# The experts of a gated trunk chosen one token tile after the other, and expert 0 gathered by itself

## The chip, the core and the metric

The kernel runs as one program on one core of a Trainium2 chip. The metric is the device time of an execution in microseconds. Five engines work from instruction queues of their own: TensorE (PE in the profile, with its weight loads shown as PEld), VectorE (DVE), ScalarE (ACT), GpSimd (POOL) and SyncE (SP), which issues nearly all of the transfers here. The DMA engines move the data.

## The reference

A decoder trunk of two layers on 256 tokens of width 1024. Layer 0 mixes tokens by forgetting attention, layer 1 by retention; after each mixer stands a mixture of experts, which is what the change is about. Its core:

```
def hier_moe(h, wr_g, br_g, wr_e, br_e, w_gu, w_down):
    p_group = softmax(xf @ wr_g + br_g)              # 4 groups
    pg, gi = top_k(p_group, 1)
    e_logits = (xf @ wr_e + br_e).reshape(T, 4, 8)   # 8 experts in each
    e_in = e_logits of the group gi
    pv, pi = top_k(softmax(e_in), 2)
    gates = pg * pv / sum(pv)
    expert_id = gi * 8 + pi
    return grouped_experts(...)   # (silu(x @ gate_e) * (x @ up_e)) @ w_down[e], times the gate, summed

for i in range(2):
    h = h + (forgetting_attention, retention)[i](rms_norm(h, norm_mix[i]), ...)
    hn = rms_norm(h, norm_ffn[i])
    h = h + hier_moe(hn, ...)
return rms_norm(h, norm_final)
```

All 32 experts of a layer have weights of their own, 6 MB each in float32 (4 MB for gate and up, 2 MB down), so that the expert weights of both layers are most of the 460 MB that the kernel reads.

## The kernel before

The 256 tokens are two tiles of 128 rows, t = 0 and 1. The residual stream `h` stays in SBUF as two tiles of 128 x 1024. The program is written in the order in which each engine runs it; nothing is scheduled afterwards.

Weights come through `Stream`: 26 slots of 1 MB, filled in a fixed order by SyncE (line 166). A load can be issued when a slot is free and the loads ahead of it have been issued; a slot is given back by the last instruction that reads it. The experts' loads stand in that list in the order of use, so that by the time a layer's gate is reached the slots hold the weights of experts 0 to 3 and a part of 4, and the next load needs a slot that expert 0 gives back. The first experts are cut into pieces of 1 MB: four for gate and up, two for down.

A layer's gate goes as follows. The last projection adds its halves to `h` (`add_h`, line 522). `Gate.transposes(n)` takes the squares of the rows on ScalarE (line 382), transposes `h` on TensorE (line 399) and copies it to `xg` (VectorE for tile 0, ScalarE for tile 1); for the second half it calls `row_rstd`, which forms 1/rms of both tiles: a sum (line 387) and a scaling (line 390) on VectorE and a power on GpSimd (line 391). `Gate.products(n)` multiplies by the router's weights (line 565) into one PSUM bank for both tiles. Then `phase_moe` starts. Nine matmuls of ones by ones (`keep_warm`, line 528) keep TensorE running. VectorE chooses the group and the two experts of each token (lines 927 to 944): logits, the largest eight, `match_replace` to mark the largest, equality, a mask over the experts of the other groups, the largest eight again, and `mkf`, the choice as zeros and ones. Each of these is written for tile 0 and tile 1 next to each other, and some are one operation for both. Three small matmuls (lines 946 to 948) count the tokens of each expert, `rk` (line 950) is the place of a token in its expert's list, and `one_hots(0)` (lines 954 and 956) makes matrices that pick up to 32 tokens for each of the four experts of a group, already scaled by rstd.

`gather` collects these rows: per half of the width two matmuls with a one-hot as the stationary operand and 512 columns of `h` (line 967), a copy on ScalarE (line 968), four transposes (line 974) and a multiplication by the norm's gain on VectorE (line 975). The result `xg` holds the inputs of the four experts side by side, 32 columns each.

Then the experts run one by one (`expert`): the gate and up product in four parts (line 1044, 16 matmuls a part), the activation on ScalarE (line 1053), its product on VectorE (line 1054), a transpose, and the down product (line 1072). Behind part 0 of expert 0 the gate values are computed (`gates`, lines 991 to 1008). The gather for the next group of four stands behind the third expert of a group.

Of the kernel before, what the change touches and what calls it, by code (L numbers as in the profile page):

```python
# [14 lines left out]
BF16 = mybir.dt.bfloat16  # L15
I32 = mybir.dt.int32
AF = mybir.ActivationFunctionType
ALU = mybir.AluOpType
# [209 lines left out]
def trunk(ctx, tc, x, fox_w_in, fox_b_f, fox_w_out, ret_w_in, ret_gn_gain, ret_w_out,  # L228
# [301 lines left out]
    class Gate:  # L530
# [3 lines left out]
        def __init__(self, l):  # L534
# [7 lines left out]
            self.top = r.new(2, 16)  # L542
            self.bank = None
            V.memset(self.L, BIG)

        def transposes(self, n):
# [10 lines left out]
            if n == 1:  # L557
                row_rstd()

        def products(self, n):  # L560
            if n == 0:
                self.bank = bank("pt")
            for t in range(2):
                for c in range(4):
                    mm(self.bank[:, 64 * t:64 * t + 36], self.xg[:, 4 * t + c, :],
                       wr[:, 4 * n + c, :], start=n == 0 and t == 0 and c == 0, stop=n == 1 and c == 3,
                       skip_group_check=True)


    def phase_a():  # L570
# [340 lines left out]
        g.products(1)  # L911
# [5 lines left out]
    def phase_moe(l, g, reserve_after, ahead, before_last, between):  # L917
# [3 lines left out]
        el, ng, rk, ex, den = r.new(2, 32), r.new(2, 4), r.new(2, NE), r.new(2, 37), r.new(2)  # L921
        gatef, gdiv, mc, gr, nrf, gs = r.new(2, NE), r.new(2, NE), r.new(1), r.new(7), r.new(1), r.new(4)
        mkf = cp.tile([P, 2, NE], BF16, name="mkf")
        keep_warm(9)
        for t in range(2):
            b = g.bank[:, 64 * t:64 * t + 36]
            V.scalar_tensor_tensor(L[:, t, 38:42], b[:, 0:4], rstd[:, t:t + 1], rb[:, 0:4], ALU.mult, ALU.add)
        for t in range(2):
            V.max(top[:, t, 8:16], L[:, t, 38:49])
        for t in range(2):  # L930
            b = g.bank[:, 64 * t:64 * t + 36]
            V.scalar_tensor_tensor(el[:, t, :], b[:, 4:36], rstd[:, t:t + 1], rb[:, 4:36], ALU.mult, ALU.add)
        for t in range(2):
            V.match_replace(Lr[:, t, 38:49], top[:, t, 8:16], L[:, t, 38:49], -BIG)
        V.tensor_tensor(ng, Lr[:, :, 38:42], L[:, :, 38:42], ALU.is_equal)
        for t in range(2):
            V.scalar_tensor_tensor(L[:, t, 0:32].rearrange("p (g e) -> p g e", g=4),
                                   ng[:, t, :, None].to_broadcast([P, 4, 8]), NEG,
                                   el[:, t, :].rearrange("p (g e) -> p g e", g=4), ALU.mult, ALU.add)
        for t in range(2):  # L940
            V.max(top[:, t, 0:8], L[:, t, 0:38])
        for t in range(2):
            V.match_replace(Lr[:, t, 0:38], top[:, t, 0:8], L[:, t, 0:38], -BIG)
        V.tensor_tensor(mkf, Lr[:, :, 0:32], L[:, :, 0:32], ALU.not_equal)
# [7 lines left out]
        def one_hots(g4):  # L952

            V.tensor_tensor(oh, rk[:, :, 4 * g4:4 * g4 + 4, None].to_broadcast([P, 2, 4, CAP]),
                            iota[:, None, None, :].to_broadcast([P, 2, 4, CAP]), ALU.is_equal)
            V.tensor_tensor(oh, oh, rstd[:, :, None, None].to_broadcast([P, 2, 4, CAP]), ALU.mult)  # L956
# [26 lines left out]
        one_hots(0)  # L983
        gather(g.xg, "acc", "acc")
# [280 lines left out]
    def phase_c():  # L1265
# [233 lines left out]
        g.products(1)  # L1499
# [78 lines left out]
```

## Time and profile before

| | us |
|---|---|
| median of three runs | 1248.16 |
| the three runs | 1246.19, 1248.60, 1248.16 |
| the profiled execution's own time | 1251.0 |
| its span in the profile | 1248.9 |
| TensorE busy in the span | 982.5 (79%) |
| VectorE busy | 414.3 (33%) |
| ScalarE busy | 317.6 (25%) |
| mean rate of the DMA over the span | 370 GB/s |

A profile is one execution. A busy share is an average over stages that have different limits: attention (0 to about 160 us), the first layer's experts (to about 590), retention (to about 806), the second layer's experts. So a change has to be read in its own stage. The releaser that stands behind an idle time is inferred: it is the event that came last.

### The profile page before, as it was taken

The numbers are of one execution on the slowest core, as the hardware profiler recorded it, in microseconds if no ns is written. First come the engines' busy times: TensorE is split into PE (matmuls) and PEld (weight loads), VectorE is DVE, ScalarE is ACT, GpSimd is POOL, SyncE is SP. The second block draws the span as 40 slices with busy tenths as digits, with TensorE's granted clock in tenths as the row PEclk, the third lists the DMA queues.
The fourth block names the chain that finished last, engine by engine and source line by source line (L and its number), as shares of the span: only waits on it lengthen the run. The fifth ranks groups of instructions, "written<-read, shape, count | busy, mean of one in ns | idle before, by whom it ended". The sixth has DMA issues, their size and how long they took to land.

```text
span 1248.9 us, 21544 instructions
## 1 busy us (share of the span) xinstructions
PE 982.5 (79%) x9223; PEld 634.3 (51%) x9223; DVE 414.3 (33%) x927; ACT 317.6 (25%) x672; POOL 42.8 (3%) x49
## 2 busy tenths in 40 slices
PE   8999986777575756678999999977776767677777
PEld 8888863343232323334889888744332323233333
DVE  5676832121111111111677676422121111111112
ACT  5665621111010100100554575321110111010112
POOL 2000000000000000000133100000000000000000
PEclk9999999899887879898999999989999888888979
DMA  9975879999999999999992768889999999999995
GB/s 339 321 264 192 321 279 421 419 427 426 427 426 427 428 428 426 427 426 394 378 335 69 268 237 308 332 357 419 423 427 428 427 427 427 427 427 427 428 424 192
DMA packets 74406, 462.20 MB, mean 370 GB/s; under 512 B 8881, under 2 KB 13761, under 8 KB 42050
## 3 DMA queue, kind: packets, MB, share of 16 engines
q1 hardware_dynamic: 73600, 460.17, 90.8%
q8 instruction: 74, 1.21, 0.4%
q10 hardware_dynamic: 706, 0.60, 0.2%
q14 instruction: 26, 0.21, 0.0%
HBM read 459.70 MB, written 1.05 MB: 369 GB/s over the span
## 4 chain that ended last, share of the span: by engine, by line
DMA 49%; PE 29%; DVE 2%; issue 1%; ACT 1%; POOLq 0%; ACTq 0%; SPq 0%; DVEq 0%
DMA slot<-in_expert_w_gu_dram 29%; DMA slot<-in_expert_w_down_dram 19%; PE sc L1044 5%; PE acc L495 4%; PE acc L509 3%; PE acc L507 3%; PE acc L508 3%; PE o L1072 3%; PE sc L967 1%; PE acc L1098 1%; DMA slot<-in_ret_w_in_dram 1%; DVE slot L1087 1%; PE pt L528 0%; PE acc L1138 0%; ACT slot L1085 0%
## 5 line engine op out<-in xcount | busy, mean ns | idle before, releaser
L1044 PE MATMUL sc<-slot,slot 128*32 128x256 f32 x4096 | 277.4, 422 | 54.9 <-DMA slot<-in_expert_w_gu_dram 51.8
L1044 PEld LDWEIGHTS sc<-slot,slot 128*32 128x32 f32 x4096 | 138.5, 119 | 181.4 <-issue 69.6
L1072 PE MATMUL o<-slot,slot 128*32 128x256 f32 x1984 | 137.8, 422 | 101.4 <-DMA slot<-in_expert_w_down_dram 58.7
L1072 PEld LDWEIGHTS o<-slot,slot 128*32 128x32 f32 x1984 | 70.8, 119 | 164.8 <-issue 80.2
L1054 DVE TENSOR_TENSOR slot<-slot,sc 128x128 f32<-128x128 f32 x64 | 23.7, 371 | 388.2 <-ACT slot L1053 388.2
L462 DVE SCALAR_TENSOR_TENSOR slot<-slot,gT,slot 128x512 fp32r<-128x512 f32 x160 | 123.9, 794 | 52.3 <-ACT slot L451 50.9
L495 PE MATMUL acc<-slot,slot 128*128 128x256 f32 x960 | 125.8, 288 | 1.6 <-ACT slot L451 1.1
L451 ACT ACTIVATE slot<-slot,gT 128x512 fp32r<-128x512 f32 x160 | 111.4, 718 | 38.6 <-PE acc L495 15.4
L495 PEld LDWEIGHTS acc<-slot,slot 128*128 128x128 f32 x960 | 118.9, 193 | 4.2 <-ACT slot L451 1.7
L1087 DVE COPY slot<-o 32x256 f32<-32x256 f32 x124 | 51.8, 418 | 204.3 <-PE o L1072 177.1
L1085 ACT ACTIVATE slot<-o 32x256 f32<-32x256 f32 x124 | 46.5, 375 | 281.5 <-DVE slot L1087 281.5
L1053 ACT ACTIVATE slot<-sc 128x128 f32<-128x128 f32 x64 | 17.7, 277 | 374.4 <-PE sc L1044 374.4
L507 PE MATMUL acc<-slot,slot 128*128 128x512 f32 x256 | 102.5, 400 | 0.0
L508 PE MATMUL acc<-slot,slot 128*128 128x512 f32 x256 | 100.0, 391 | 2.1 <-DVE slot L462 2.1
L509 PE MATMUL acc<-slot,slot 128*128 128x512 f32 x256 | 100.1, 391 | 0.0
L967 PE MATMUL sc<-h,slot 128*128 128x512 f32 x112 | 72.8, 811 | 33.5 <-DVE slot L956 33.5
L1098 PE MATMUL acc<-slot,slot 128*128 128x512 f32 (+1 forms) x128 | 60.9, 611 | 13.4 <-ACT slot L1085 13.2
L967 PEld LDWEIGHTS sc<-h,slot 128*128 128x128 f32 x112 | 27.7, 258 | 74.6 <-issue 74.6
L508 PEld LDWEIGHTS acc<-slot,slot 128*128 128x128 f32 x256 | 48.2, 188 | 11.8 <-DVE slot L462 2.8
L509 PEld LDWEIGHTS acc<-slot,slot 128*128 128x128 f32 x256 | 48.0, 188 | 10.2
L507 PEld LDWEIGHTS acc<-slot,slot 128*128 128x128 f32 x256 | 48.2, 188 | 9.3 <-issue 0.3
L975 DVE TENSOR_TENSOR slot<-pt,gT 128x512 f32<-128x512 f32 x28 | 19.4, 691 | 96.5 <-PE pt L974 96.5
(237 smaller groups left out, 750.6 us busy)
## 6 DMA issues: line engine op xcount, KB each, us to landing
slot<-in_expert_w_gu_dram SPq DMA_DIRECT2D x84, 2048.0 KB, 39.1
slot<-in_expert_w_gu_dram SPq DMA_DIRECT2D x86, 1024.0 KB, 13.4
slot<-in_expert_w_down_dram SPq DMA_DIRECT2D x42, 2048.0 KB, 39.1
slot<-in_expert_w_down_dram SPq DMA_DIRECT2D x40, 1024.0 KB, 13.3
slot<-in_ret_w_in_dram SPq DMA_DIRECT2D x24, 1024.0 KB, 14.1
slot<-in_fox_w_in_dram SPq DMA_DIRECT2D x15, 1024.0 KB, 11.8
slot<-in_ret_w_out_dram SPq DMA_DIRECT2D x8, 1024.0 KB, 7.3
slot<-in_fox_w_out_dram SPq DMA_DIRECT2D x4, 1024.0 KB, 14.6
```

What stands on the lines that cost most here:

```text
L451: A.activation(wh, w, AF.Copy, scale=1.0 if g is None else g)
L462: V.scalar_tensor_tensor(wl, w, g, wh, ALU.mult, ALU.subtract)
L495: mm(o, w[:, P * j:P * j + P], x[:, k, :], start=first and k == 0 and j % 2 == 0, stop=last and k == 7, skip_group_check=True)
L507: mm(banks[t], xh[:, q], wh, start=first and k == ks[0], stop=False)
L508: mm(banks[t], xh[:, q], wl, start=False, stop=False)
L509: mm(banks[t], xl[:, q], wh, start=False, stop=last and k == ks[-1])
L967: mm(b, o[:, t, :], h[:, t, 512 * n:512 * n + 512], start=t == 0, stop=t == 1)
L1044: mm(bgu[32 * j:32 * j + 32, 0:256].rearrange("p (two f) -> p two f", two=2), xg[:, kk, 32 * e4:32 * e4 + 32], wv[:, :, P * j:P * j + P], ...
L1072: mm(by[32 * nb:32 * nb + 32, 0:256], gTt[:, 32 * j:32 * j + 32], w[:, j % n, 256 * nb:256 * nb + 256], start=j == 0, stop=j == 3, skip_gr ...
L1085: A.activation(o, i, AF.Copy)
L1087: V.tensor_copy(o, i)
L1098: mm(sums[t, n], w2["scm"][0:rows, P * t:P * t + P], y4[0:rows, 512 * n:512 * n + 512], start=start, stop=False, skip_group_check=True)
```

## The change

There are three parts, the same in both layers.

The choice of experts moves from `phase_moe` into the gate and goes tile by tile. The router's products of the two tiles go to two PSUM banks. Where the last half of `h` is multiplied, the order is now: products of tile 0, rstd of tile 0 (`tile_rstd`, operations on one column), the group of tile 0, rstd of tile 1, the experts of tile 0, products of tile 1, the group and the experts of tile 1. Of the nine `keep_warm` matmuls ahead of the count six are left, in another bank.

Expert 0 gets an input of its own, `x0`: two one-hots of 32 columns, and sixteen matmuls that take a strided block of `h` as the stationary operand and give the transposed rows at once; VectorE multiplies them by the gain, one half of the width after the other. The one-hots of experts 1 to 3 follow.

The gather of the whole group is moved behind expert 0's gate and up product, ahead of its down product.

```diff
+    def tile_rstd(t):
+        V.tensor_tensor(st_[:, t:t + 1], ss[:, 0, t:t + 1], ss[:, 1, t:t + 1], ALU.add)
+        V.tensor_scalar(st_[:, t:t + 1], st_[:, t:t + 1], 1.0 / D, EPS, ALU.mult, ALU.add)
+        G.tensor_tensor(rstd[:, t:t + 1], st_[:, t:t + 1], mhalf[:, 0:1], ALU.pow)
...
-        g.products(1)
+        g.products(1, (0,))
+        tile_rstd(0)
+        g.groups(0)
+        tile_rstd(1)
+        g.experts(0)
+        g.products(1, (1,))
+        g.groups(1)
+        g.experts(1)
...
-        keep_warm(9)
...
+        keep_warm(6, "acc")
         b = bank("sc")
         mm(b[:, 0:32], trb, mkf[:, 0, :], start=True, stop=True, skip_group_check=True)
         mm(b[:, 32:64], onb, mkf[:, 0, :], start=False, stop=False, skip_group_check=True)
         mm(b[:, 32:64], trb, mkf[:, 1, :], start=False, stop=True, skip_group_check=True)
-        keep_warm(3)
+        keep_warm(3, "acc")
...
-        one_hots(0)
-        gather(g.xg, "acc", "acc")
+        x0 = g.xg[:, 0:2, :].rearrange("p a (k s) -> p (a k) s", s=CAP)
+        for t in range(2):
+            V.tensor_scalar(oh[:, t, 0, :], iota, rk[:, t, 0:1], rstd[:, t:t + 1], ALU.is_equal, ALU.mult)
+        bx = bank("acc")[:, 0:8 * CAP].rearrange("p (k s) -> p k s", k=8)
+        for n in range(2):
+            for c in range(4):
+                for t in range(2):
+                    hv = h[:, t, 512 * n:512 * n + 512].rearrange("p (q c) -> p c q", c=4)
+                    mm(bx[:, 4 * n + c, :], hv[:, c, :], oh[:, t, 0, :], start=n == 0 and c == 0 and t == 0,
+                       stop=t == 1, skip_group_check=True)
+            V.tensor_tensor(x0[:, 4 * n:4 * n + 4, :], bx[:, 4 * n:4 * n + 4, :],
+                            gT[:, gi, 4 * n:4 * n + 4, None].to_broadcast([P, 4, CAP]), ALU.mult)
+        one_hots(0, 1)
...
-            gg, gTt = first_product(e, e4, xg, after_part)
+            gg, gTt = first_product(e, e4, xg if e else x0, after_part)
             turned(gg, gTt)
+            if e == 0:
+                gather(xg, "acc", "acc")
             by = bank("o")
```

VectorE's row at the end of attention, from rstd to the choice of experts, before (`st_` is the mean square, `top`, the logits and the marks are parts of one slot):

```order
L387 TENSOR_TENSOR st__85<-ss 128x2
L390 TENSOR_SCALAR st__85<-st__85 128x2
L927 SCALAR_TENSOR_TENSOR slot_124<-pt,rstd,rb 128x4 x2
L929 MAX slot_124<-slot_124 128x8 x2
L932 SCALAR_TENSOR_TENSOR slot_124<-pt,rstd,rb 128x32 x2
L934 MATCH_REPLACE slot_124<-slot_124 128x11 x2
L935 TENSOR_TENSOR slot_124<-slot_124 128x8
L937 SCALAR_TENSOR_TENSOR slot_124<-slot_124 128x32 x2
L941 MAX slot_124<-slot_124 128x8 x2
L943 MATCH_REPLACE slot_124<-slot_124 128x38 x2
L944 TENSOR_TENSOR mkf<-slot_124 128x64
```

The same engine and place, now:

```order
L395 TENSOR_TENSOR st__85<-ss 128x1
L396 TENSOR_SCALAR st__85<-st__85 128x1
L577 SCALAR_TENSOR_TENSOR slot_124<-pt,rstd,rb 128x4
L578 MAX slot_124<-slot_124 128x8
L579 SCALAR_TENSOR_TENSOR slot_124<-pt,rstd,rb 128x32
L580 MATCH_REPLACE slot_124<-slot_124 128x11
L581 TENSOR_TENSOR slot_124<-slot_124 128x4
L395 TENSOR_TENSOR st__85<-ss 128x1
L396 TENSOR_SCALAR st__85<-st__85 128x1
L586 SCALAR_TENSOR_TENSOR slot_124<-slot_124 128x32
L589 MAX slot_124<-slot_124 128x8
L590 MATCH_REPLACE slot_124<-slot_124 128x38
```

Tile 0's choice (line 591) follows, and then the nine operations of tile 1, from line 577 to line 591 again; what stood in pairs stands in two rows one after the other.

TensorE's row from the count of tokens to expert 0's down product, before:

```order
L948 MATMUL sc<-mkf,trb 128x32
L528 MATMUL o<-ones 128x128 x3
L967 MATMUL acc<-h,slot_124 128x512 x4
L974 MATMUL acc<-ident,slot_124 128x128 x8
L987 LDWEIGHTS onb
L987 MATMUL sc<-mkf,onb 128x32
L988 LDWEIGHTS onb
L988 MATMUL sc<-mkf,onb 128x32
L1044 MATMUL sc<-slot_135,slot_124 32x256 x8
L1044 MATMUL sc<-slot_137,slot_124 32x256 x8
L1044 MATMUL sc<-slot_139,slot_124 32x256 x8
```

And now, with what each waits for, expert 0's narrow gather being line 1005 and its gate and up product line 1069:

```order
L959 MATMUL sc<-mkf,trb 128x32 [waits DVE_49]
L534 MATMUL acc<-ones 128x128 x3
L1005 MATMUL acc<-slot_124,h 128x32 [waits DVE_49] x2
L1005 MATMUL acc<-slot_124,h 128x32 x6
L1005 MATMUL acc<-slot_124,h 128x32 [waits DVE_49]
L1005 MATMUL acc<-slot_124,h 128x32 x7
L1012 LDWEIGHTS onb
L1012 MATMUL sc<-mkf,onb 128x32
L1013 LDWEIGHTS onb
L1013 MATMUL sc<-mkf,onb 128x32
L1069 MATMUL sc<-slot_135,slot_124 32x256 [waits DMAHW5_49,DMAHW1_49,PE_49]
L1069 MATMUL sc<-slot_135,slot_124 32x256 x7
```

The wide gather has left the row ahead of the first product, and the narrow one has a wait for VectorE at its ninth matmul, where its second half begins. Further on in the same row, behind the last part of expert 0's first product:

```order
L1069 MATMUL sc<-slot_989,slot_124 32x256 x7
L980 MATMUL acc<-h,slot_124 128x512 [waits DVE_49]
L980 MATMUL acc<-h,slot_124 128x512
L980 MATMUL acc<-h,slot_124 128x512 [waits PE_49]
L980 MATMUL acc<-h,slot_124 128x512
L987 MATMUL acc<-ident,slot_124 128x128 [waits Activation_49]
L987 MATMUL acc<-ident,slot_124 128x128 x3
L987 MATMUL acc<-ident,slot_124 128x128 [waits Activation_49]
L987 MATMUL acc<-ident,slot_124 128x128 x3
L1099 MATMUL o<-slot_991,slot_989 32x256 [waits DMAHW5_49,DVE_49]
L1099 MATMUL o<-slot_991,slot_989 32x256 x7
```

Here the wide gather (lines 980 and 987) stands now between expert 0's first product and its down product (line 1099).

## Rows read from the trace of the kernel before

**Rows 1.** Stages: length; busy PE, PEld, DVE, ACT, POOL; PEclk; DMA share; GB/s.
```profile
168.50:175.00 6.50, 6.22 (x46) 3.57 (x50) 1.66 (x5) 2.72 (x4) 0.00 (x0) 1.00 0.01 4
175.00:181.00 6.00, 4.80 (x92) 3.02 (x88) 2.92 (x14) 1.67 (x4) 0.00 (x0) 1.00 0.89 321
181.00:590.00 409.00, 282.95 (x3160) 142.18 (x3152) 66.01 (x160) 42.90 (x114) 0.00 (x0) 0.89 1.01 424
...
808.50:815.00 6.50, 6.22 (x54) 3.63 (x56) 2.03 (x8) 3.19 (x5) 0.00 (x0) 1.00 0.01 3
```

**Rows 2.** The chain that ended last, shares of the span by line.
```profile
DMA slot<-in_expert_w_gu_dram 29%; DMA slot<-in_expert_w_down_dram 19%; PE sc L1044 5%; PE acc L495 4%; PE acc L509 3%; PE acc L507 3%; PE acc L508 3%; PE o L1072 3%; PE sc L967 1%; PE acc L1098 1%; DMA slot<-in_ret_w_in_dram 1%; DVE slot L1087 1%; PE pt L528 0%; PE acc L1138 0%; ACT slot L1085 0%
```

**Rows 3.** Order of time, layer 0's gate: start us, us, instruction, [idle before <-releaser].
```profile
160.16 1.38 DVE L522 TENSOR_TENSOR h<-h,acc 128x512 f32<-128x512 f32 x2 [4.98 <-PE acc L509]
...
162.99 0.69 POOL L391 TENSOR_TENSOR rstd<-st__85,mhalf 128x2 f32<-128x2 f32 x1 [116.43 <-DVE st__85 L390]
...
164.25 0.35 DVE L927 SCALAR_TENSOR_TENSOR slot<-pt,rstd,rb 128x4 f32<-128x4 f32 x2 [1.44 <-PE pt L565]
...
165.04 0.08 DVE L934 MATCH_VALUE_LOAD slot<-slot 128x8 f32 x1
...
166.56 0.22 DVE L944 TENSOR_TENSOR mkf<-slot 128x64 bf16<-128x64 f32 x1
```

**Rows 4.** Order of time, from the rank to expert 0's first product.
```profile
167.24 0.23 DVE L950 SCALAR_TENSOR_TENSOR slot<-sc,mkf 128x64 f32<-128x64 f32 x1 [0.46 <-PE sc L948]
...
167.96 0.42 DVE L956 TENSOR_TENSOR slot<-slot,rstd 128x256 f32<-128x256 f32 x1
...
168.44 3.70 PE L967 MATMUL acc<-h,slot 128*128 128x512 f32 x8 [0.60 <-DVE slot L956]
...
173.36 0.11 PEld L987 LDWEIGHTS <-onb 128*128 128x128 bf16 x1
...
173.61 3.66 PE L1044 MATMUL sc<-slot,slot 128*32 128x256 f32 x64
```

**Rows 5.** SyncE's loads around expert 0, and one kind's size and count.
```profile
161.22 15.94 SPq L166 DMA_DIRECT2D slot<-in_expert_w_gu_dram  x4
179.59 2.05 SPq L166 DMA_DIRECT2D slot<-in_expert_w_down_dram  x2
...
slot<-in_expert_w_gu_dram SPq DMA_DIRECT2D x86, 1024.0 KB, 13.4
```

**Rows 6.** Order of time: the router's products, and the product behind the activation.
```profile
162.18 1.96 PE L565 MATMUL pt<-wr,slot 128*128 128x36 f32 x16
...
177.65 0.37 DVE L1054 TENSOR_TENSOR slot<-slot,sc 128x128 f32<-128x128 f32 x1 [0.50 <-ACT slot L1053]
```

**Rows 7.** GpSimd's power by line: count, ns min/median/max, first and last start, form.
```profile
L391 POOL TENSOR_TENSOR rstd<-st__85,mhalf x5: 693/699/1137, 19.6 to 1242.3; 128x2 f32<-128x2 f32 x5
...
L1363 POOL TENSOR_TENSOR rs<-rs,mhalf x8: 921/922/1066, 646.0 to 713.3; 128x1 f32<-128x1 f32 x8
```

**Rows 8.** Order of time: two operations of the gate values, each needing the last.
```profile
175.05 0.16 DVE L996 TENSOR_REDUCE slot<-slot 128x2 f32<-128x8 f32 x1 [0.33 <-ACT slot L995]
175.25 0.16 DVE L997 SCALAR_TENSOR_TENSOR slot<-slot 128x2 f32<-128x2 f32 x1
```

**Rows 9.** Order of time, layer 1: the choice, and expert 0's first product.
```profile
806.20 0.23 DVE L944 TENSOR_TENSOR mkf<-slot 128x64 bf16<-128x64 f32 x1
...
813.12 3.66 PE L1044 MATMUL sc<-slot,slot 128*32 128x256 f32 x64
```

**Rows 10.** Order of time: three of the fourteen gathers of later groups.
```profile
198.49 3.67 PE L967 MATMUL sc<-h,slot 128*128 128x512 f32 x8 [2.40 <-DVE slot L956]
...
245.74 5.37 PE L967 MATMUL sc<-h,slot 128*128 128x512 f32 x8 [2.40 <-DVE slot L956]
...
1163.30 5.37 PE L967 MATMUL sc<-h,slot 128*128 128x512 f32 x8 [2.40 <-DVE slot L956]
```

**Rows 11.** Stages, TensorE alone: length; PE busy; PEclk; DMA share; GB/s.
```profile
245.80:249.10 3.30, 3.30 (x4) 0.50 1.02 425
```

More of the change, by code (lines that the diff above doesn't have):

```diff
@@ L542, in __init__ @@
             self.top = r.new(2, 16)
+            self.el, self.ng = r.new(2, 32), r.new(2, 4)
+            self.mkf = cp.tile([P, 2, NE], BF16, name="mkf")
             self.bank = None
@@ L556, in transposes, with products, groups, experts @@
             h_transposed(n, "sc", evict)
-            if n == 1:
-                row_rstd()
-        def products(self, n):
+        def products(self, n, ts=(0, 1)):
             if n == 0:
-                self.bank = bank("pt")
-            for t in range(2):
+                self.bank = [bank("pt"), bank("o")]
+            for t in ts:
                 for c in range(4):
-                    mm(self.bank[:, 64 * t:64 * t + 36], self.xg[:, 4 * t + c, :],
-                       wr[:, 4 * n + c, :], start=n == 0 and t == 0 and c == 0, stop=n == 1 and c == 3,
-                       skip_group_check=True)
+                    mm(self.bank[t][:, 0:36], self.xg[:, 4 * t + c, :], wr[:, 4 * n + c, :],
+                       start=n == 0 and c == 0, stop=n == 1 and c == 3)
+        def groups(self, t):
+            L, Lr, top, b = self.L, self.Lr, self.top, self.bank[t]
+            V.scalar_tensor_tensor(L[:, t, 38:42], b[:, 0:4], rstd[:, t:t + 1], rb[:, 0:4], ALU.mult, ALU.add)
+            V.max(top[:, t, 8:16], L[:, t, 38:49])
+            V.scalar_tensor_tensor(self.el[:, t, :], b[:, 4:36], rstd[:, t:t + 1], rb[:, 4:36], ALU.mult, ALU.add)
+            V.match_replace(Lr[:, t, 38:49], top[:, t, 8:16], L[:, t, 38:49], -BIG)
+            V.tensor_tensor(self.ng[:, t, :], Lr[:, t, 38:42], L[:, t, 38:42], ALU.is_equal)
+        def experts(self, t):
+            L, Lr, top = self.L, self.Lr, self.top
+            V.scalar_tensor_tensor(L[:, t, 0:32].rearrange("p (g e) -> p g e", g=4),
+                                   self.ng[:, t, :, None].to_broadcast([P, 4, 8]), NEG,
+                                   self.el[:, t, :].rearrange("p (g e) -> p g e", g=4), ALU.mult, ALU.add)
+            V.max(top[:, t, 0:8], L[:, t, 0:38])
+            V.match_replace(Lr[:, t, 0:38], top[:, t, 0:8], L[:, t, 0:38], -BIG)
+            V.tensor_tensor(self.mkf[:, t, :], Lr[:, t, 0:32], L[:, t, 0:32], ALU.not_equal)
     def phase_a():
@@ L920, in phase_moe @@
         L, Lr, top, oh = g.L, g.Lr, g.top, g.oh
-        el, ng, rk, ex, den = r.new(2, 32), r.new(2, 4), r.new(2, NE), r.new(2, 37), r.new(2)
+        rk, ex, den = r.new(2, NE), r.new(2, 37), r.new(2)
         gatef, gdiv, mc, gr, nrf, gs = r.new(2, NE), r.new(2, NE), r.new(1), r.new(7), r.new(1), r.new(4)
-        mkf = cp.tile([P, 2, NE], BF16, name="mkf")
-        keep_warm(9)
[L925 to L944, printed above, removed]
+        mkf = g.mkf
+        keep_warm(6, "acc")
         b = bank("sc")
@@ L1498, in phase_c @@
         g.transposes(1)
-        g.products(1)
+        g.products(1, (0,))
+        tile_rstd(0)
+        g.groups(0)
+        tile_rstd(1)
+        g.experts(0)
+        g.products(1, (1,))
+        g.groups(1)
+        g.experts(1)
         yield g
```

10 lines of the change are left out of this document (6 added, 4 removed).

## The prediction

> **What bounds the kernel now.** I read the stages first [rows 1]. In the first expert phase (181 to 590 us; the second looks the same) the DMA share is 1.01 at 424 GB/s: expert weights arrive as fast as they can, TensorE is busy 283 of 409 us, and nothing that an engine does there moves the end. The projections ahead of each expert phase are not touched by the change. What remains are two short holes, one at the start of each expert phase: from 168.5 to 175 us and from 808.5 to 815 us the DMA moves 3 to 4 GB/s. There all slots are full, and the next load waits until expert 0's first product has used up a slot. The chain of waits says the same in sum: 29 and 19% of the span are the transfers of the two expert weights [rows 2]. So a hole is the place where the change counts, and it counts one for one: a microsecond by which expert 0 starts later is a microsecond without transfers, the bytes behind it are the same, and the phase ends later by it. Afterwards I looked at what fills the hole: the gate's small VectorE operations [rows 3], the ranks and the gather [rows 4], and the loads behind expert 0 [rows 5].
>
> **The change, part by part, in layer 0.** Expert 0's first matmul stands at 173.61 us now [rows 4].
>
> *Start of the gate.* Now rstd of both tiles is one GpSimd operation, 162.99 to 163.68, and the first router operation on VectorE starts at 164.25, when the products of the second tile are done (162.18 + 1.96 [rows 6]). Afterwards the first tile needs only its own half of the products, so rstd ends its wait. GpSimd's price is open: two columns took 0.69 us, but the same operation on one column, which is what the new helper issues, took 0.92 us in all of its eight runs [rows 7]. I take 0.92, the row of the same shape: 162.99 + 0.92 + 0.1 = 164.0, a gain of 0.25 us (0.45 with 0.69).
>
> *The chain of choices.* Now the two tiles go side by side: while the result of one is on its way, the other's operation fills the pipe, and both choices take 164.25 to 166.78, 2.53 us [rows 3]. Afterwards the order has tile 0's nine operations, then tile 1's. What a lone operation costs when the next needs its result is shown further down in the same phase: a start every 0.20 us for tiny ones (175.05, 175.25) [rows 8]; on 32 columns I take 0.22. One tile is then seven such steps (first logits, maximum, match, equality, mask, maximum, match, choice), 1.55 us, plus two value loads of 0.08 [rows 3] and the last operation of 0.2: 1.9 us. In tile 0's stretch stand also the two operations for tile 1's rstd, 0.2 us, so tile 0 is chosen at 164.0 + 2.1 = 166.1. Tile 1's rstd leaves VectorE at about 165.2 and needs 0.92 us on GpSimd and some 0.3 on the way there and back, ready at 166.4; then 1.9 us more: 168.3. **The choice of both tiles ends 1.5 us later than now** (1.1 with the cheaper GpSimd), since two chains in a row replace two side by side; TensorE's products, which are to hide the first, end by 164.14 anyway [rows 6].
>
> *Ranks and one-hots.* Now from the choice (166.78) to the gather's first matmul (168.44) it is 1.66 us: 0.46 to the rank, 0.26 for it, 0.88 for two operations over 256 elements, 0.06 to TensorE [rows 4]. Afterwards only one small matmul stands behind the last choice, 0.4, then 0.26, then two operations over 32 elements. No row shows that form; half of the 0.35 us that a pair of small ones takes [rows 3] bounds one below, the 0.26 from rank to one-hot [rows 4] above, and I take 0.2 for the first one, with the second hidden behind the first matmul; 0.06 to TensorE. Sum 0.92: a gain of 0.75. TensorE starts at 169.2. Of the clock-keeping matmuls six stay ahead of the ranks and three behind; the three run beside VectorE's one-hots, as now.
>
> *The gather.* Now 168.44 to 173.61, 5.17 us: four wide matmuls, copies, eight transposes, scaling [rows 4]. Afterwards sixteen matmuls with h as the stationary operand and 32 columns, each in two passes as the router's are: 16 passes of the router's took 1.96 us with their drain [rows 6]. The order shows that the second half waits for VectorE to have read the first half out of the same bank; that wait is on the path: 0.1 to VectorE, 0.37 for a 128 x 128 operation from PSUM [rows 6], 0.06 back. So 2.0 + 0.53 + 1.8 for the second half, whose drain the next weights hide, + 0.25 for the two count matmuls and the first weights as now: 4.6 us, a gain of 0.6. Bounds: 4.1 if the wait were hidden, 5.0 if strided weights take as long as their slowest neighbour.
> The Trainium skill (TensorE: Matmul & The Clock Gate, LDWEIGHTS) says that loading weights takes time by their columns alone, however little they are then used; that rule speaks against this part, and an estimate by its 107 ns for 128 columns is 3.4 us for the 32 passes. The row, at about 0.12 us a pass, is close to it and is what the sum uses; by the page expert 0 would start 0.4 us earlier per layer.
>
> *Sum at full clock.* 169.2 + 4.6 = 173.85 against 173.61: **+0.25 us** in layer 0. Layer 1's gate takes 6.69 us from the end of the choice (806.43) to expert 0 (813.12) [rows 9], where layer 0's takes 6.83; I take +0.3 there. Together +0.55.
>
> *The clock.* Between the end of the six clock-keeping matmuls (12 passes of at most the router's 0.12 us [rows 6], 1.5 us: from 164.0 to 165.5) and the last rank matmul at 168.4 TensorE has two tiny matmuls to do in 2.9 us. Now its wait ahead of the gather is 0.6 us [rows 4]. What a wait like that does can be seen at the gathers of the later groups, 14 in all, each behind a wait of 2.4 us: two of them (the first at 198.49) took 3.67 us; the others, from 245.74 to 1163.30, 5.37 or more [rows 10]. During the one at 245.74 the granted clock was 0.50, the 1.2 GHz of the two levels [rows 11]. Price: 1.7 us, on a gather of about the length of the new one. Those gathers also have idle stretches ahead of their wait, while here TensorE comes from dense projections; so I take not 12 in 14 but 6 in 10 a layer. One of the two layers is then the likeliest: +1.7.
> [...]
>
> *Behind expert 0.* The wide gather for experts 1 to 3 now stands between expert 0's first and second product. It costs TensorE about 4.9 us (168.44 to 173.36 now, with its copies [rows 4]), less the moment in which it idles there now, so expert 1 starts 3 to 5 us later. Who waits: SyncE's queue, whose next load needs a slot of the second product. Now three loads of 1 MB are issued during expert 0 and the fourth at 179.59 [rows 5]. By the stages [rows 1] 321 GB/s x 6 us, 1.9 MB, had moved at 181 us, and the other 1.2 MB last until 183.9, 10.3 us after expert 0's start. Afterwards the second product starts 3.5 + 4.9 = 8.4 us after it, and the fourth load is issued half a second product later, at 9.5 us. 0.8 us are left: I cost this at nothing; cover gone, it would cost what is missing, up to 1 us a layer. VectorE gets the other three experts' one-hots (two operations of up to 0.42 [rows 4]) ahead of the gate values in place of the scaling of the wide gather, which moves behind; it idles 0.50 us ahead of expert 0's activation product now [rows 6], so this is hidden.
>
> **Sum.** +0.55 + 1.7 = +2.25 us on the profiled execution's 1251.0 us (span 1248.9 and 2.1 around it). That execution is 2.8 us over the median of 1248.16, so the same step from the median gives **1250.4 us**.
>
> **Rivals.** *The clock falls in both layers*: +0.55 + 3.4, **1252.1**, slower. For: the 12 of 14. Against: the dense work ahead of the gate. It decides from an idle stretch of about 2.4 us on. *It falls in neither*: +0.55, **1248.7**. For: in the hole now the clock stays at 1.00. *The loads run dry behind the wide gather*: one fall and 1 us a layer, **1252.4**; decides when the second product starts over 9.2 us after expert 0 does. *The shorter path wins*: GpSimd at 0.69, the bank wait hidden, no fall: 0.7 us gained a layer, **1246.8**; for it speaks that the gather and the one-hots are truly shorter, against it the eight rows at 0.92 and the wait in the order. Only with more overlap than that, which no row shows, would it be faster by over 0.2%.
>
> **How the numbers follow.** About 0.2%, 2.5 us, is what a measurement of this kernel can tell from no change: the three runs shown span 2.4 us. Chances: one fall 0.42, both 0.26, neither 0.14, dry loads 0.07, shorter path 0.11. One fall lies just inside 0.2%, and a quarter to a third of it beyond; with both and dry loads slower gets 0.41. Faster gets 0.10, most of the shorter path with the runs' own spread; the same 0.49. The range takes from the shorter path to both falls with half a microsecond: 1246.8 to 1252.8.
>
> **What would show it.** Right: the second tile's choice ends some 4 us after the first router operation; GpSimd's rstd takes 0.9 us twice; the narrow gather has a gap of half a microsecond in its middle; expert 0 starts 13.7 us after the last pair of additions to h begins (now 173.61 - 160.16 = 13.45 [rows 3, 4]), or 15.4 with a fall; the clock row of that stretch shows 0.50 in one layer. Wrong: expert 0 earlier than 13 us after that add, a choice of both tiles in under 3 us, or a second hole in the DMA row some 10 us behind expert 0's start.

## The result, and the profile after

| | before | after |
|---|---|---|
| median, us | 1247.78 (4 runs, 1246.19 to 1248.6) | 1258.69 (4 runs, 1257.65 to 1259.7) |
| span of the profiled execution | 1248.9 | 1258.0 |
| ratio of the medians | | 1.009, 95% interval 1.0075 to 1.0105 |

The change costs 10.9 us. The forecast was 1250.4 with a range up to 1252.8: the sign of the likeliest case was right, the size was missed by 8 us, and the time lies outside the range.

The stages of after that answer to [rows 1], with the stretches behind them (length; busy PE, PEld, DVE, ACT, POOL; granted clock; DMA share; GB/s). The two executions differ by chance ahead of the gate: the transposes of layer 0 start at 159.12 us here and at 160.90 in before (two rows, before and after), and starts are counted from there below.

```profile
160.90 1.44 PE L399 MATMUL sc<-ident,h 128*128 128x128 f32 x8
...
159.12 1.44 PE L405 MATMUL sc<-ident,h 128*128 128x128 f32 x8
```

```profile
168.50:175.00 6.50, 6.12 (x30) 5.80 (x34) 0.58 (x3) 0.00 (x0) 0.00 (x0) 0.50 0.00 0
175.00:181.00 6.00, 6.00 (x65) 2.65 (x57) 2.73 (x17) 1.55 (x2) 0.00 (x0) 0.57 0.56 182
181.00:190.00 9.00, 8.72 (x94) 4.96 (x93) 2.90 (x6) 2.23 (x5) 0.00 (x0) 1.00 0.77 287
190.00:590.00 400.00, 278.09 (x3109) 139.26 (x3102) 65.59 (x159) 42.24 (x112) 0.00 (x0) 0.89 1.01 425
808.50:815.00 6.50, 4.91 (x29) 4.61 (x27) 2.67 (x16) 0.00 (x0) 0.20 (x1) 0.74 0.44 182
815.00:822.00 7.00, 6.62 (x45) 5.30 (x48) 1.98 (x10) 0.85 (x2) 0.00 (x0) 0.50 0.00 0
822.00:835.00 13.00, 12.72 (x136) 6.72 (x132) 4.24 (x14) 2.92 (x6) 0.00 (x0) 0.87 0.78 277
```

Three things stand in these rows. The granted clock, 1.00 in the holes of before, is 0.50 in both layers, the 1.2 GHz of the two levels. The hole lasts longer: the DMA share from 175 to 181 us is 0.56, where before had 0.89. And behind it is a second, shallower hole, 0.77 from 181 to 190, where before had 1.01. From 190 us on everything is as it was, 1.01 at 425 GB/s. So the whole loss is made at the start of each expert phase. The traces agree on the sum: from layer 0's transposes to layer 1's it is 645.2 us in after and 639.6 in before (+5.6), from there to the end 453.7 and 448.4 (+5.3).

What fills the hole now, in order of time (start, us, instruction, idle time before it and what ended that):

```profile
161.09 0.56 POOL L397 TENSOR_TENSOR rstd<-st__85,mhalf 128x1 f32<-128x1 f32 x1 [117.12 <-ACT slot L559]
161.68 0.22 DVE L577 SCALAR_TENSOR_TENSOR slot<-pt,rstd,rb 128x4 f32<-128x4 f32 x1 [0.76 <-POOL rstd L397]
...
165.33 0.19 DVE L591 TENSOR_TENSOR mkf<-slot 128x32 bf16<-128x32 f32 x1
165.57 0.18 PE L959 MATMUL sc<-mkf,trb 128*128 128x32 bf16 x1 [1.59 <-DVE mkf L591]
...
166.41 3.94 PE L1005 MATMUL acc<-slot,h 128*128 128x32 f32 x16
...
170.73 3.94 PE L1005 MATMUL acc<-slot,h 128*128 128x32 f32 x16 [0.38 <-DVE slot L1007]
...
174.66 6.37 PE L1069 MATMUL sc<-slot,slot 128*32 128x256 f32 x64
...
180.96 3.70 PE L980 MATMUL acc<-h,slot 128*128 128x512 f32 x8
...
186.08 1.94 PE L1099 MATMUL o<-slot,slot 128*32 128x256 f32 x32
...
187.22 2.06 SPq L166 DMA_DIRECT2D slot<-in_expert_w_down_dram  x2
```

L1005 is the narrow gather, L1069 expert 0's gate and up product, L980 the moved wide gather, L1099 expert 0's down product. Against [rows 3, 4], counted from the first transpose: both tiles are chosen after 6.40 us (before 5.88), and expert 0 starts after 15.54 us (before 12.71). Of these 2.83 us the choice took 0.52, the ranks and one-hots gave back 0.77 (0.89 us from the choice to the gather, before 1.66), and the gather, up to expert 0's first matmul, added 3.08 (8.25 us, before 5.17). Expert 0's product then lasts 6.37 us in place of 3.66. Layer 1 reads the same: 15.49 and 6.35 us, in before 12.58 and 3.66. The later start and the longer product make 5.5 us in layer 0 and 5.6 in layer 1, together the loss.

### The profile page after: what moved, and what is told of

Read it like the earlier page. It is cut to its first block, busy times and chain, and to the rows that moved or that the text cites. A ratio compares the mean times of both kernels' runs of the same rounds, so it can differ in the third digit from the quotient of the medians.

```text
span 1258.0 us, 21668 instructions
## 1 busy us (share of the span) xinstructions
PE 994.3 (79%) x9275; PEld 644.2 (51%) x9275; DVE 417.6 (33%) x943; ACT 317.5 (25%) x672; POOL 42.8 (3%) x51
## 5 line engine op out<-in xcount | busy, mean ns | idle before, releaser
L1069 PE MATMUL sc<-slot,slot 128*32 128x256 f32 x4096 | 283.8, 430 | 54.8 <-DMA slot<-in_expert_w_gu_dram 54.1
L1069 PEld LDWEIGHTS sc<-slot,slot 128*32 128x32 f32 x4096 | 140.5, 121 | 184.7 <-issue 69.7
L1099 PE MATMUL o<-slot,slot 128*32 128x256 f32 x1984 | 132.4, 410 | 97.1 <-DMA slot<-in_expert_w_down_dram 52.2
L1099 PEld LDWEIGHTS o<-slot,slot 128*32 128x32 f32 x1984 | 68.0, 116 | 158.6 <-issue 68.1
L980 PE MATMUL sc<-h,slot 128*128 128x512 f32 x112 | 73.5, 818 | 33.5 <-DVE slot L968 33.5
L980 PEld LDWEIGHTS sc<-h,slot 128*128 128x128 f32 x112 | 28.1, 262 | 75.8 <-issue 75.8
```

What stands on the lines that cost most here:

```text
L980: mm(b, o[:, t, :], h[:, t, 512 * n:512 * n + 512], start=t == 0, stop=t == 1)
L1069: mm(bgu[32 * j:32 * j + 32, 0:256].rearrange("p (two f) -> p two f", two=2), xg[:, kk, 32 * e4:32 * e4 + 32], wv[:, :, P * j:P * j + P], ...
L1099: mm(by[32 * nb:32 * nb + 32, 0:256], gTt[:, 32 * j:32 * j + 32], w[:, j % n, 256 * nb:256 * nb + 256], start=j == 0, stop=j == 3, skip_gr ...
```

## The experiments

All ratios are against runs of the kernel before on the same chip (median 1246.6 to 1246.8 us). Three theories stood at first: that the narrow gather lets the clock fall and stay low (the thin gather), that the longer choice does it, and that the moved wide gather starves the loads.

**The choice alone.** The old gather is back, the choice stays tile by tile.

```diff
-        x0 = g.xg[:, 0:2, :].rearrange("p a (k s) -> p (a k) s", s=CAP)
...
-        one_hots(0, 1)
+        one_hots(0)
+        gather(g.xg, "acc", "acc")
...
-            if e == 0:
-                gather(xg, "acc", "acc")
```

> The changed kernel with the old gather put back: the choice tile by tile stays, the wide gather stands ahead of expert 0 again. The theory of the thin gather (the narrow gather keeps the clock low): no narrow gather, so expert 0's first product lasts 3.7 us as before; the choice ends about 0.5 us later (6.40 against 5.88 us after the transposes) and, if the granted clock falls in the wait for tile 1's choice, the wide gather lasts 5.37 us instead of 3.70 (both lengths stand in the trace of before): 0.5 to 2.2 us a layer, 1249 to 1252.5. The theory of the choice (the wait of 1.59 us on the mask of tile 1 makes the clock fall, and that is where the loss comes from): a granted clock of 0.50 behind the choice and most of the loss still there, 1254 to 1258. The theory of the moved gather (the wide gather between expert 0's products starves the loads): 1248 to 1249.5, and one hole in the loads per layer, as before.

Measured: 1248.13 us, ratio 1.001 (1.000 to 1.002). In order of time, layer 0:

```profile
166.91 5.40 PE L980 MATMUL acc<-h,slot 128*128 128x512 f32 x8 [0.47 <-DVE slot L968]
...
173.77 3.66 PE L1058 MATMUL sc<-slot,slot 128*32 128x256 f32 x64
```

In layer 0 the clock did fall behind the wait of 1.59 us, to 0.56 in the mean of 167 to 170.8 us, and the wide gather lasted 5.40 us where it takes 3.70 at full clock, exactly the forecast's price of 1.7; the clock was back ahead of expert 0, which started 2.02 us later than in before. In layer 1 it did not fall, and expert 0 started 0.43 us later. The choice costs 1.3 us (0 to 2.5), about a tenth of the loss. It is not the main cause.

**The gather alone.** The choice of before, with the narrow gather and the moved wide one.

```diff
-        one_hots(0)
-        gather(g.xg, "acc", "acc")
+        x0 = g.xg[:, 0:2, :].rearrange("p a (k s) -> p (a k) s", s=CAP)
...
+        one_hots(0, 1)
...
+            if e == 0:
+                gather(xg, "acc", "acc")
```

> The kernel before with the narrow gather and the moved wide gather, the choice as it was. Theory of the thin gather: the clock falls all the same, in the narrow gather or behind it, its halves last 2 to 3.9 us each and expert 0's first product up to 6.4: 1254 to 1258. Theory of the choice: the clock stays at 1.00, each half lasts about 2.0 us, the first product 3.7, the fourth load is issued about 10 us behind expert 0's start, when the first three have just landed: 1247 to 1249. Theory of the moved gather: clock 1.00 or not, a second hole in the loads per layer, 2 us each: 1251 to 1253.

Measured: 1259.14 us, ratio 1.0096 (1.0079 to 1.0113). All of the loss is here. The gather and the product behind it in order of time:

```profile
166.13 3.94 PE L993 MATMUL acc<-slot,h 128*128 128x32 f32 x16
170.46 3.94 PE L993 MATMUL acc<-slot,h 128*128 128x32 f32 x16 [0.38 <-DVE slot L995]
...
174.38 6.17 PE L1057 MATMUL sc<-slot,slot 128*32 128x256 f32 x64
```

TensorE in three stretches of it (length; PE busy; granted clock; DMA share; GB/s):

```profile
166.20:169.20 3.00, 3.00 (x14) 1.00 0.05 22
169.40:174.40 5.00, 4.62 (x24) 0.50 0.00 0
174.40:179.40 5.00, 5.00 (x51) 0.50 0.40 118
```

The loads of the gather's weights over the whole run (count; least, median and longest in ns; first and last start):

```profile
L993 PEld LDWEIGHTS acc<-slot,h x64: 308/329/332, 166.1 to 818.4; 128*128 128x128 f32 x64
```

This upset all three theories. The first half of the gather, 166.13 to 170.07 us, stands for the most part at a granted clock of 1.00 (from 166.2 to 169.2 throughout) and lasts 3.94 us, as long as the second at 0.50. A half is 16 passes, of which the last by itself takes 0.42 us, so one follows the other after (3.94 - 0.42) / 15 = 0.23 us at either clock, where the forecast had 0.12. So a fourth theory: the weights are a strided view of `h`, every fourth column, and loading them takes twice the time. The trace of before had a pair of rows that says so, the weight loads of two kinds of transposes, L1031 from adjoining columns and L974 from every fourth (columns as above):

```profile
L1031 PEld LDWEIGHTS pt<-ident,slot x32: 137/142/224, 188.9 to 1207.7; 128*128 128x128 f32 x32
...
L974 PEld LDWEIGHTS pt<-ident,slot x112: 195/209/220, 201.6 to 1170.4; 128*128 128x128 f32 x112
```

The Trainium skill (Advanced Engine Details and Errata, SBUF Cachelines) says that SBUF is read in lines of 16 bytes and that accesses which each touch another line are penalised; every fourth float32 is a line of its own. These rows agree, 209 against 142 ns. The section of the Trainium skill that the forecast used (TensorE: Matmul & The Clock Gate, LDWEIGHTS) prices a load by its columns alone and does not speak of their stride; for these loads that differs from the measurement, 0.23 us against 0.107, and the measurement decides.

**The choice's wait filled.** Six more products of ones stand where TensorE waited 1.59 us.

```diff
         mm(b[:, 32:64], onb, mkf[:, 0, :], start=False, stop=False, skip_group_check=True)
+        keep_warm(6, "acc")
```

> The changed kernel with six more products of ones by ones (some 1.6 us) put between the two counts of tile 0's mask and the count of tile 1's, where TensorE waited 1.59 us. Theory of the choice: no wait, no fall; narrow halves of 2.0 us and a first product of 3.7: 1247 to 1249. Theory of the thin gather: the clock falls some us later, inside the narrow gather or in expert 0's first product: 1252 to 1258. Theory of the moved gather: 1252 to 1254 with the clock at 1.00 and two holes in the loads per layer.

Measured: 1258.97 us, ratio 1.01 (1.0078 to 1.0122). TensorE in order of time, from the last count to expert 0:

```profile
165.44 0.18 PE L960 MATMUL sc<-mkf,trb 128*128 128x32 bf16 x1 [0.16 <-DVE mkf L591]
...
166.27 3.94 PE L1006 MATMUL acc<-slot,h 128*128 128x32 f32 x16
170.60 3.94 PE L1006 MATMUL acc<-slot,h 128*128 128x32 f32 x16 [0.39 <-DVE slot L1008]
...
174.52 6.09 PE L1070 MATMUL sc<-slot,slot 128*32 128x256 f32 x64
```

The wait is gone (0.16 us). The clock still stands at 1.00 from 166.3 to 169 us, but falls all the same inside the gather (0.52 in the mean of 170 to 180 us), and nothing is won.

**The wide gather later.** It stands behind expert 0's down product.

```diff
             gg, gTt = first_product(e, e4, xg if e else x0, after_part)
             turned(gg, gTt)
-            if e == 0:
-                gather(xg, "acc", "acc")
...
                 if j == 1 and e >= WARM:
                     keep_warm(2, "sc")
+            if e == 0:
+                gather(xg, "acc", "acc")
```

> The changed kernel with the wide gather put behind all of expert 0's second product instead of ahead of it. The clock is left as it is: the theories of the thin gather and of the choice expect it at 0.50 for some 13 us again, the first hole as long as in the changed kernel, but the fourth load issued some 5 us earlier, so that the second hole (2.1 us a layer in the DMA share) goes: 1253.5 to 1256. Theory of the moved gather: all of the loss was in the second hole: 1247 to 1249.

Measured: 1257.97 us, ratio 1.0086 (1.007 to 1.0103), not to be told from the change. In order of time, SyncE's fourth load and expert 1's first product:

```profile
182.48 7.33 SPq L166 DMA_DIRECT2D slot<-in_expert_w_down_dram  x2
...
188.35 3.66 PE L1069 MATMUL sc<-slot,slot 128*32 128x256 f32 x64
```

The fourth load is issued 22.8 us after the transposes instead of 28.1, but expert 1 starts where it did (28.6 against 28.7), so the loads behind that one wait all the same. The expectation of 2 us a layer from the second hole failed.

**Adjoining columns.** One line of the changed kernel.

```diff
-                    hv = h[:, t, 512 * n:512 * n + 512].rearrange("p (q c) -> p c q", c=4)
-                    mm(bx[:, 4 * n + c, :], hv[:, c, :], oh[:, t, 0, :], start=n == 0 and c == 0 and t == 0,
+                    c0 = 512 * n + P * c
+                    mm(bx[:, 4 * n + c, :], h[:, t, c0:c0 + P], oh[:, t, 0, :], start=n == 0 and c == 0 and t == 0,
```

> The changed kernel, but the narrow gather takes its 128x128 weights from adjoining columns of h instead of every fourth one. The rows of expert 0's input then stand in another order than its weights: expert 0's outputs are wrong, no work is left out. Theory of the stride (a weight load from every fourth column takes 0.233 us instead of 0.112, at either clock; the run with the gather alone had passes 0.233 us apart while the granted clock was still 1.00): the halves last 1.8 to 2.1 us instead of 3.94; with the clock at 1.00 behind them 1247 to 1249, with a fall into expert 0's first product 1249.5 to 1252.5. Theory of the clock alone (the halves are long because the clock is at 0.50): halves of 3.9 us, 1257 to 1259.

Measured: 1255.03 us, ratio 1.0073 (1.0051 to 1.0095). In order of time:

```profile
166.56 1.97 PE L1005 MATMUL acc<-slot,h 128*128 128x32 f32 x16
168.91 3.62 PE L1005 MATMUL acc<-slot,h 128*128 128x32 f32 x16 [0.38 <-DVE slot L1007]
...
172.52 5.19 PE L1069 MATMUL sc<-slot,slot 128*32 128x256 f32 x64
```

The same two halves as stretches of TensorE (columns as above):

```profile
166.50:168.60 2.10, 2.03 (x18) 1.00 0.00 0
169.00:172.40 3.40, 3.40 (x17) 0.50 0.00 0
```

The first half, at full clock, lasts 1.97 us, the forecast's 2.0, and with the strided view it lasts 3.94 at full clock too (the gather alone): the stride is shown. The second half, behind the fall, lasts 3.62: at 0.50 a pass from adjoining columns is nearly as slow as a strided one. So the two causes cover each other, and taking one away brings only part. The time expected for this case (up to 1252.5) was missed; the four runs lie in two pairs, near 1252.7 and 1257.1, the profile is of the lower, and what the upper does is open.

**128 columns, strided.** From the gather alone: all four experts' one-hots (`o`) move over the same strided weights, into two banks without a wait between the halves, and the wide gather is still done.

```diff
+        o = oh.rearrange("p t e s -> p t (e s)")
...
-                    mm(bx[:, 4 * n + c, :], hv[:, c, :], oh[:, t, 0, :], start=n == 0 and c == 0 and t == 0,
+                    mm(bx[:, c, :], hv[:, c, :], o[:, t, :], start=c == 0 and t == 0, stop=t == 1,
...
```

> The run with the gather alone (old choice), the gather of expert 0 now with all four experts' one-hot columns moving: 128 columns a pass instead of 32, the weights from every fourth column as in the changed kernel; the wide gather is still done, unneeded, ahead of expert 0's second product. Theory of the stride: the passes stay 0.233 us apart, the halves 3.7 to 4.0 us; with four times the columns the clock stays at 1.00, expert 0's first product lasts 3.7 instead of 6.2 us, and of these 2.5 us a layer some part comes back: 1254 to 1257.5. Theory of the clock alone: passes of 0.13 us (as the products of ones by ones), halves of 2.1 us, 1248 to 1250.

Measured: 1256.04 us, ratio 1.0072 (1.0055 to 1.0089). In order of time:

```profile
166.27 7.73 PE L992 MATMUL acc<-slot,h 128*128 128x128 f32 x32 [0.60 <-DVE slot L957]
...
173.97 3.66 PE L1055 MATMUL sc<-slot,slot 128*32 128x256 f32 x64
```

As stretches of TensorE, the gather and expert 0's product:

```profile
166.30:174.00 7.70, 7.70 (x38) 0.78 0.00 0
174.00:177.60 3.60, 3.60 (x68) 1.00 0.45 109
```

As the theory of the stride has it: the passes stay 0.23 us apart (median weight load 329 ns), though each does four times the work. The clock falls for a part of the gather, which costs these loads nothing, and is back at 1.00 for expert 0's product, which lasts 3.66 us. That takes 3 us off the time of the gather alone. Expert 0 starts as late in both (15.24 and 15.21 us after the transposes, in layer 1 15.11 and 15.06), so these 3 us come from the product behind the gather: the part of the loss that is the low clock. What is left, 9 us, is lateness of 2.5 us in each layer.

**Both away.** The same with adjoining columns.

```diff
-                    hv = h[:, t, 512 * n:512 * n + 512].rearrange("p (q c) -> p c q", c=4)
-                    mm(bx[:, c, :], hv[:, c, :], o[:, t, :], start=c == 0 and t == 0, stop=t == 1,
+                    c0 = 512 * n + P * c
+                    mm(bx[:, c, :], h[:, t, c0:c0 + P], o[:, t, :], start=c == 0 and t == 0, stop=t == 1,
```

> The run with 128 columns moving (old choice, wide gather still done ahead of expert 0's second product), now with the weights from adjoining columns of h: both suspects, the stride and the low clock, are away, only the moved wide gather is left. Expert 0's rows stand in another order than its weights: its outputs are wrong, no work is left out. Passes 0.12 us apart, 3.84 us in all, expert 0's first product 3.7 us long and 11.3 to 11.5 us behind the transposes (12.71 before); the wide gather then holds back expert 0's second product by some 3.9 us, so that expert 1 starts about 2.7 us later than in the kernel before. Theory that the stride and the clock were all of the loss (the prediction's: the moved gather costs nothing): 1245 to 1247. Theory that TensorE's time up to expert 1 counts, whatever it is spent on (some 0.6 us for each us and layer): 1248.5 to 1250.5.

Measured: 1247.02 us, ratio 1.0001 (0.9991 to 1.0011). In order of time, from the gather to expert 1:

```profile
166.03 3.84 PE L992 MATMUL acc<-slot,h 128*128 128x128 f32 x32 [0.60 <-DVE slot L957]
...
169.84 3.66 PE L1055 MATMUL sc<-slot,slot 128*32 128x256 f32 x64
173.44 3.70 PE L969 MATMUL acc<-h,slot 128*128 128x512 f32 x8
...
180.31 3.64 PE L1055 MATMUL sc<-slot,slot 128*32 128x256 f32 x64
```

The gather's stretch of TensorE had a granted clock of 1.00 throughout (166 to 169.8 us), and its weight loads over the whole run were:

```profile
L992 PEld LDWEIGHTS acc<-slot,h x64: 186/192/193, 166.0 to 807.7; 128*128 128x128 f32 x64
```

The whole loss is gone, with the wide gather still between expert 0's products, and the stride of the weights is all that differs from the run before: a load takes 192 ns where the strided one took 329, and expert 0 starts 11.34 us after the transposes where it started 15.24. The moved gather by itself costs nothing that can be measured: the gather without transposes, two experiments further down, does without it, starts expert 0 as early (11.35 us) and has the same ratio.

**Lateness by itself.** The kernel before, with eleven products of ones ahead of expert 0.

```diff
+        keep_warm(11, "acc")
         def start(part):
```

> The kernel before with eleven products of ones by ones (2.9 us at full clock) ahead of expert 0's first product in each layer, nothing else: the price of being late, by itself. If there are 0.8 us of slack and then every us counts, as the prediction took it: 4.2 us, 1250.5 to 1251.5. If 0.6 us of each counts: 3.4 us, 1249.5 to 1250.5. If the loads have slack for all of it: 1246 to 1247. If there is none: 5.8 us, 1252 to 1253.

Measured: 1254.14 us, ratio 1.0059 (1.0043 to 1.0076). Expert 0 starts 15.25 and 15.12 us after the transposes, 2.54 later than in before, at full clock and with the old gather.

```profile
171.44 2.70 PE L528 MATMUL acc<-ones 128*128 128x128 f32 x22
174.07 3.66 PE L1044 MATMUL sc<-slot,slot 128*32 128x256 f32 x64
```

5.1 us late in both layers cost 7.3 us (5.4 to 9.5): at least one for one, and more than any of the four expectations; why more is open. There is no slack ahead of expert 0. The 9 us of the 128 strided columns, just as late, agree with it within their intervals (6.9 to 11.1).

**A gather without transposes.** If adjoining columns make the weights cheap, one gather with h as the weights can serve all four experts; their gate and up weights and the norm's gain are then loaded in that order of rows, and no other gather is needed for them.

```diff
-        gather(g.xg, "acc", "acc")
...
+        for n in range(2):
...
+            for c in range(4):
+                for t in range(2):
+                    c0 = 512 * n + P * c
+                    mm(bx[:, c, :], h[:, t, c0:c0 + P], o[:, t, :], start=c == 0 and t == 0, stop=t == 1,
+                       skip_group_check=True)
...
-            gu = w_gu[l, e].rearrange("(n p c) f -> n p c f", n=2, c=4)
+            gu = w_gu[l, e].rearrange("(n p c) f -> n p c f" if e >= 4 else "(n c p) f -> n p c f", n=2, c=4)
```

> The kernel before; only the gather of the first four experts is other: h's adjoining columns as weights and the 128 one-hot columns moving, which gives the gathered rows transposed at once, with no eviction, no transposes and no second gather; the four experts' gate and up weights are loaded with their rows in that order (pieces of 4 KB instead of 8 KB), and the gain likewise. Theory of the stride: 32 passes 0.13 us apart, 4.2 us from the one-hots to expert 0's first product where the old gather took 5.17: 1.0 us a layer earlier, 1245 to 1247. Rivals: the passes are 0.233 us apart all the same (then it is not the stride): 7.5 us, 1251 to 1253; the smaller pieces slow the loads: 1248 to 1251.

Measured: 1246.82 us, ratio 1.0001 (0.9992 to 1.0011). The gather lasts 3.84 us and expert 0 starts 1.36 us earlier in each layer, yet the time does not move. To see whether the smaller pieces of the loads eat it, they were put alone into the kernel before:

> The kernel before, only the gate and up weights of the first four experts of each layer loaded in pieces of 4 KB instead of 8 KB, with their rows in another order (those experts' outputs are wrong, no work is left out). If the smaller pieces are why the gather without transposes brought nothing: 1248 to 1250. If they cost nothing: 1246 to 1247.5, and that stays open.

Measured: 1247.51 us, ratio 1.0003 (0.9992 to 1.0013): at most 1.6 us, nothing measurable. Why 2.7 us of earliness bring nothing there stays open.

**The same, tile by tile.** Here the change's first idea gets work to hide behind: tile 0's ranks, one-hots and half of the gather run while VectorE chooses for tile 1. `rank(t)` makes the ranks and one-hots of tile t, `take(t, n)` is tile t's share in half n of the gather. Against the changed kernel:

```diff
+        rank(0)
+        g.experts(1)
+        take(0, 0)
         mm(b[:, 32:64], trb, mkf[:, 1, :], start=False, stop=True, skip_group_check=True)
-        keep_warm(3, "acc")
...
+        rank(1)
+        take(0, 1)
+        for n in range(2):
+            take(1, n)
...
```

> The gather of the run before this one, with the choice tile by tile: tile 0's ranks, one-hots and its half of the gather are done while VectorE chooses for tile 1. Theory of the stride, and the gate as a chain: expert 0's first product some 10.6 to 11.1 us behind the transposes instead of 12.71, the clock held by the products that now fill TensorE's wait: 1243 to 1245.5. Rivals: VectorE's order (tile 0's one-hots ahead of tile 1's choice) eats the gain: 1246 to 1248; the clock falls in the choice: 1248 to 1251.

Measured: 1244.25 us, ratio 0.9971 (0.9957 to 0.9984). The same kernel once more:

> The gather without transposes with the choice tile by tile, again, in more rounds beside the others: 0.995 to 0.999 of the kernel before if the first measurement held; 0.999 to 1.001 if it was the chip.

Measured: 1243.89 us, ratio 0.9976 (0.9967 to 0.9984). This beats both kernels. TensorE in layer 0, in order of time:

```profile
164.86 1.16 PE L970 MATMUL acc<-slot,h 128*128 128x128 f32 x8 [1.36 <-DVE slot L965]
...
165.85 0.18 PE L978 MATMUL sc<-mkf,trb 128*128 128x32 bf16 x1
165.88 3.15 PE L970 MATMUL acc<-slot,h 128*128 128x128 f32 x24
...
169.00 3.66 PE L1079 MATMUL sc<-slot,slot 128*32 128x256 f32 x64
```

Expert 0 starts 10.36 us after the transposes instead of 12.71 (layer 1: 10.33, 12.58). Behind the last count (L978) the rest of the gather goes without a gap.

## Why the prediction was wrong

The step that failed is **the gather**: its sum took a pass from the router's row, 0.12 us, and gave 4.6 us up to expert 0; it measured 8.25. The router's weights are adjoining columns, the gather's are every fourth. The adjoining-column run shows the forecast's own figure (1.97 us for a half at full clock), and every strided run shows 3.92 to 3.94 for a half of 32-column passes. A gain of 0.6 us was forecast, a loss of 3.08 measured. The upper bound in that paragraph, 5.0 "if strided weights take as long as their slowest neighbour", had no row behind it; the two kinds of transposes in the trace of before would have given one, 209 against 142 ns.

**The clock** was rightly named as a cost, with the wrong size and only a part of the reason. It was priced as one wide gather at 0.50, 1.7 us, and once in two layers. It fell in both and stayed for 13.6 us (here TensorE in after: length; PE busy; granted clock; DMA share; GB/s):

```profile
159.00:166.60 7.60, 5.92 (x47) 1.00 0.85 321
166.60:180.20 13.60, 13.22 (x86) 0.50 0.20 64
180.20:190.00 9.80, 9.52 (x106) 1.00 0.78 290
```

So it covers expert 0's product too, 6.37 us for 3.66, a term that the sum does not have; in the strided gather, which the forecast would have charged, it costs nothing. The prediction looked for the cause in the wait of the choice; with the wait filled, or with the old choice, the clock falls as well. The work that followed was what differed: behind the gathers of 32 columns expert 0's product began at 0.50, behind those of 128 at 1.00. The narrow gathers also have a wait of 0.38 us in their middle, which those of 128 columns lack; no run parts the two, and why the clock stays low is open. That the sign of the forecast came out right is partly luck: it rested on one fall, while the gather, the larger loss, was told as a gain.

By what was taken away, the loss reads: both causes away, +0.2 us; with the stride, +9; with the stride and the low clock in expert 0's product, +12 for the gather alone. The tile-by-tile choice adds nothing to that (10.9 us in the change, against other runs of before, 12.2 with its wait filled, 12.3 with the old choice).

**Start of the gate**: GpSimd's operation on one column took 0.56 us, not 0.92; the row of the same shape [rows 7] misled, and the one of the same line (0.69) was nearer. The first router operation came 0.79 us earlier, not 0.25. **The chain of choices** was near: 3.84 us from its first operation to the last choice, where the sum has 4.3 (164.0 to 168.3). Together the choice ended 0.52 us later, not 1.5. **Ranks and one-hots**: 0.89 us, told 0.92. **The bank wait**: TensorE idled 0.38 us, told 0.53. Two slips in the sums change nothing: 169.2 + 4.6 is 173.8, not 173.85, and both falls with half a microsecond end at 1252.6, not 1252.8.

**Behind expert 0**: in the change the cover was gone, since expert 0's product took 2.7 us longer: the fourth load came 12.6 us after expert 0's start, not 9.5, and the second hole was there, as the rival of the dry loads has it. But that is a consequence: with both causes away the fourth load came 9.9 us after expert 0's start, and the moved gather cost nothing, as forecast. **One for one**: held for lateness, and more than held (7.3 us for 5.1). It did not hold for earliness: 4.6 us earlier in the two layers gave 3.0 us (2.0 to 4.1), 2.7 us gave nothing measurable.

The chances were laid out mostly around the clock, and none of the five cases had a slower gather. The rival of both falls, 1252.1, had the sign and the layers right; that of the dry loads, 1252.4, came nearest and is still 6 us short.

## What to carry to other kernels

Before a tensor becomes the stationary operand, look at the stride of its view, and price the weight loads by a row with that stride; four bytes in sixteen doubled them here, the one stride that was tried. Price a clock that falls by all that TensorE does until the rows show it back, not by the one operation behind the wait. And where the loads wait for a slot that one product gives back, all that is put ahead of that product counts in full; splitting a chain in two pays once the first part has work to do beside the second.

## What was not expected of the hardware

A strided pass takes 0.23 us at a granted clock of 1.00 and of 0.50 alike, while one from adjoining columns takes about 0.11 at 1.00, (1.97 - 0.28) / 15, and 0.21 at 0.50, (3.62 - 0.42) / 15; what is taken off is the length of the last pass. So the low clock is not seen in the strided gather at all, only in the product behind it. GpSimd's power took 0.56 us on one column in the gate and 0.92 in another place of the same program [rows 7]; what makes that difference was not tried.
